# Strassen's products for 24 of the 32 column blocks of a decoder layer's up projection

## The chip, the cores and the metric

The kernel runs on one core of a Trainium2 chip. The core has a matrix engine (TensorE, PE in the profile; its weight loads are PEld), a vector engine (VectorE, DVE), an engine for activations (ScalarE, ACT), a general one (GpSimd, POOL) and one that issues transfers (SyncE, SP). Each takes its own queue in order and waits for the others by semaphores. The metric is the time of one execution in microseconds (us) of device time.

## The reference

One layer of a hybrid decoder trunk: 512 tokens, width 1024. A mixer (a gated recurrent group and a sparse attention group behind one input projection) is followed by a feed-forward part, which alone is touched here:

```python
x = x + (1.0 + g1[:, None, :]) * rms_norm(y, post_norm_mix[l])
h = modulate(rms_norm(x, pre_norm_mlp[l]), sh2, sc2)
y = jnp.square(jax.nn.relu(h @ w_ff1[l])) @ w_ff2[l]
x = x + (1.0 + g2[:, None, :]) * rms_norm(y, post_norm_mlp[l])
```

h is 512 x 1024, w_ff1 (up) 1024 x 4096, w_ff2 (down) 4096 x 1024, all float32.

## The kernel before

**Precision.** Every float32 operand is split into two parts of a shorter type, hi (a rounded copy) and lo (the remainder), and `mm3` multiplies hi x hi, hi x lo and lo x hi into the same sum. `split_f32` makes the parts: a copy (on ACT or DVE) and a subtraction (on DVE or POOL). So each weight and each activation costs work on those engines before PE can use it.

**Order.** The kernel first runs its Python once with a clock of estimated costs (`Clocks`), in which streams of work (`Stream`, `run_streams`) are interleaved. This records one node for each instruction. `flush` then issues the nodes in the order that the string PLAN gives, two characters a node. Where an instruction has several possible engines (`choose`, by way of `either` and `copy`), a letter of PLACE for its stream decides: a for ACT, d for DVE, p for POOL. The letters of a stream are used up in the order in which the choices are recorded; WS is the weights' stream, TH the transposes' one, UF the first up blocks, UP the up stage, DN the down stage.

**Weights.** `Weights` holds jobs in order. Each loads 512 KB into one of 4 raw buffers and splits it into one of 4 slots of hi and lo (PART_BUFS). A job with `make` takes two slots. A slot is given back when its user drops it.

**Up projection.** h is normalised in two pairs of token tiles (256 tokens each), transposed (`turn_h`) and split into h2 and h2l, 8 tiles of 128 rows of the width. A column block f is 128 of the 4096 columns; its result is 128 x 512 (columns by tokens), the sum over 8 k-tiles of three matmuls of 512 columns. The first four blocks run in `up_first`, half the tokens at a time while the rest of the mixer ends, so in matmuls of 256 columns. The other 28 follow in `up`. `relu2` takes relu from PSUM on ACT and squares on POOL or DVE, and for the pairs below 28 also makes two sums for the down projection.

**Down projection.** It already uses Strassen's method in Winograd's form for 14 pairs of row blocks (NJ): `first_pair` and `first_ones` make the activations' and weights' combinations of the first four products, `second_pair` and `second_ones` those of the other three; four plain blocks (28 to 31) end it. All activations' parts come from `part()`, in a pool that opens when h2 is closed.

**Beside it.** `ada_row(5, ...)`, the stream G2, makes the row of the last gate: eight loads into the two `ar` tiles, two DVE steps on each, into accT.

The matmuls have line 315 in the profile, transposes 318, ACT's operations 325, all operations chosen between DVE and POOL 357, loads 399.

Of the kernel before, what the change touches and what calls it, by code (L numbers as in the profile page):

```python
# [6 lines left out]
F32 = mybir.dt.float32  # L7
# [43 lines left out]
PAIRS = (0, 1)  # L51

# [6 lines left out]
    '###*#+#-#&#(#v#3#6#8#9#:#M#P#R#U#X#?#E#H#W#^#$#)#%#,#.#/#0#L#4#1$&#{#2#7#<#K#N#Y#[#_#a#d#q#w$.$0$1$7'  # L59
    '$8$=$D$G$J$O$P$S#5#@#C#S$X#c#J#Q#V#b#k%>#O#Z#]#h#e$w#T#p#s$)$2%8#f#i#l#n#|$#$($+$9$:$<$>$?$A$B$C$H$E'  # L60
    '$U$F#t$3$5$@$Q$K$T$]#A$N#x$6$Y$j$`$W$V$Z$d$m$a$s$_$o$g$t$z%,$}$r${$b$M$[$l$p$c$e$i$n$q$~%)$-$;$R%#%$'
    '%-%1%(%%%7%*%A%9%2%0%F%:%L%=%6%4$|$k$u%+$v$^$f$h$y%.%3%D$x%/%j%O%M%c%?%@%C%P%N%e%V%G%I%R%`%h%X%Z%]%J'
    '%<%H%g%r%E%S%T%[%^%f%n%&%5%m%l%s%i&$%u%k%q%~%o&&%{%|&,&2&1&)&#%}%d%W%a%w%b%K%U%Y%_%p%v&-%B%Q&z&.&5&<'
    '&/&+&*&I&6&B&;&F&D&L&7&J&A&N&Q&0%y&%%x%z&3&4&G&9&M%t&(&v&f&h&T&Y&O&S&g&j&U&[&R&^&u&l&V&]&a&b&8&P&W&>'
    '&?&H&K&Z&_&q&@&X(#&x&o&m&i&|(9(*&y&n($&~(?(:(%(/(((A(L&c&C&p&d&e&s&t&w&}()&`&k&r(;(,(1(3(C(N(=(-(4(7'
    '(D(P(Q(Y(5(>(G(U#I(y(k)1)*(<(8(E(B(@(F(O(V#G-u#~$%(.(R&:&=(f(~);)o(H(S(M(Z(`(d(h(v)R(s(K)&)e)`(b(o(X'
    '(^)6(u(m&E&{(&(|(+)V(0)I)a*4)F)x)d*=*f+P*8*l*?*y*;*s*i+G+W,K+E,)+(+V+u,`-.([(j(l(n(a(i(t(w(z(2(6(p(q'
    '(r(}(x({)$)%)+).)#)5):)A)/)0)<)=)C(I(J(T)9)@)i#;#=#>#B#D#F#`#g#j#m#o#r(W(](_#u#z#}$$$*$,$/$4(c(e(g$I'
    '#y$L%;)))(),)-)3)4)7)8)>)?)D)E)G)J)K)L)N)S)k)t*#)B)H)P)[)^)_)b)c)f)u)})~*$*&*)*-*/*0*3*6*7*<*A*C*E)M'
    ')O)X)Z)Q)T)U)W)g)Y)]*%*.*5)q)r)v)w)h)j)n)p)z*Q*U*_)y){)|*()s***1*2*c+&+-+@+3+>*L*N*O*Y*F*P*S*T*m+I*9'  # L70
    '*:*>*@*B*D*G*H*J*K*R*V*W*X*j*k*p*r*v*w*z*}+#+%+*+/+5+9+`+n+w*a*b*e*h*q*x*{*|+$*~+}*Z*]*d*n*o*t*u+++,'
    '+4+6+7+8+:+=+?+A+D+F+H+J+K+L+U+Y,%,0,G)l)m*,*+*^*[+)+1+2+o,R,L,g,d+B+M+O+Q+R+S+T+X+Z+[+]+^+c+e+g+k+p'
    '+t+{,*,+,,,-,.,4,X-P/#,D,t0#09+a+b+j*I*M*`*g+l+m+r+_+h+v-G+s+y+~,$,&,(,1,3,5,7,9,:,=,O,],_,a,c,h,o,v'
    ',}+;+<,<,N,8,A,>,S+.+0+N+x+d+|+f+i-%-,-1-E-6-:-2-C-H,?,@,B,C,E,H,P,Q,T,U,V,Y,Z,e,f,i,k,m,s,u,x,z,{,~'
    '-(-4-;-j-$-&-*---0-5-7-<->,J,W,[,l,^,|,b,w-@-F-I+q+z,/,q,6,;,2,F-+-9-k-p-y-A-?-=-c-J-K-M-Q-R-V-W-[-^'
    '-e-h-i-o-w.,.S-B-D-N-O-S-m-Y-Z-|.&-T-U-`-b-g-q-v-x-{...m.{,n,p-)-/-#-X-~.#.%,I,M,j-L.3.6.7.8.9.G.Y/N'
    '0f.Q.T.V.W.X.a.d/(/./>.f.y0a-_-z.*.1.J.L.u.}/$.(.).-.<.A.H.2.B.M.x-3-8-a-s-]-d,r,y-f.$.0.;.@.P.I.?.R'
    '.C.O.Z._.q/-/1/4/;/G-l-n.+.:.//&-r-t-}//.].^.`.n/+/3/,/5/7/8/=/U.D.g.i.o.k.r.5.K.U.z/9/?/s/i/Q/C/E/V'
    '/:/J/M/O/H/K/R/[/W/p/q/x/*/0/A/_/L/Z.b.e/B/I/y/{0(0=0@/h/~0$0%0*0I/e/j/k/w0d0m/X/]/d/u/a/g/P/b/f/o/}'
    '0)0.050?03070+0R0^0_0g0N0P0p0r1*1+16170&000G0M18191~2W211,1;1=1>1@1H1113151D1N1h0K0Q0S0Z1O1P1Q1Y1S1T'  # L80
# [1631 lines left out]
```

## Time and profile before

| | us |
|---|---|
| median of 3 runs | 623.78 (623.05 to 623.98) |
| the profiled execution, its own time | 624.71 |
| its span, first to last instruction | 622.9 |
| mean granted TensorE clock, share of full | 0.994 |

Time outside the span is start and end of the program. The profile gives for each engine its busy time and share of the span. Rows of the order of time have start, duration, engine, line, operation, output and inputs by the program's names, shapes and a count; in square brackets stands how long the engine was idle before and what released it. Rows of a stretch of time (A:B) have the length, the busy time of PE, PEld, DVE, ACT and POOL with counts, the granted clock, the share of the transfer engines and GB/s. The busy times of instructions that overlap are counted once, while the mean duration of a group counts each in full. Matmuls are pipelined: the duration of one is longer than the distance to the next.

### The profile page before, as it was taken

The numbers are of one execution on the slowest core, as the hardware profiler recorded it, in microseconds if no ns is written. First come the engines' busy times: TensorE is split into PE (matmuls) and PEld (weight loads), VectorE is DVE, ScalarE is ACT, GpSimd is POOL, SyncE is SP. The second block draws the span as 40 slices with busy tenths as digits, with TensorE's granted clock in tenths as the row PEclk, the third lists the DMA queues.
The fourth block names the chain that finished last, engine by engine and source line by source line (L and its number), as shares of the span: only waits on it lengthen the run. The fifth ranks groups of instructions, "written<-read, shape, count | busy, mean of one in ns | idle before, by whom it ended". The sixth has DMA issues, their size and how long they took to land.

```text
span 622.9 us, 8887 instructions
## 1 busy us (share of the span) xinstructions
PE 599.3 (96%) x3072; PEld 499.8 (80%) x3072; DVE 500.1 (80%) x972; ACT 340.7 (55%) x699; POOL 204.5 (33%) x206
## 2 busy tenths in 40 slices
PE   6999999999889999999999999999998999999993
PEld 6888889967678889789888888888786788888883
DVE  5998989899998989886675617536699999998867
ACT  6546217899999999875312111121374666656412
POOL 5004012445536648323234456414400000230253
PEclk9999999999999999999999999999998999999998
DMA  8996895150019120007442322422223343443403
GB/s 352 378 321 241 318 382 193 71 209 27 17 69 351 59 105 11 1 2 253 182 174 68 124 79 68 135 86 84 68 85 128 120 137 123 153 168 103 135 1 135
DMA packets 26837, 89.03 MB, mean 143 GB/s; under 512 B 2980, under 2 KB 3236, under 8 KB 26792
## 3 DMA queue, kind: packets, MB, share of 16 engines
q1 hardware_dynamic: 26648, 88.40, 39.9%
q8 instruction: 24, 0.39, 0.3%
q14 instruction: 21, 0.17, 0.1%
q10 hardware_dynamic: 144, 0.07, 0.0%
HBM read 86.36 MB, written 2.10 MB: 142 GB/s over the span
## 4 chain that ended last, share of the span: by engine, by line
PE 88%; ACT 5%; DVE 4%; DMA 1%; issue 1%; POOLq 0%; POOL 0%; ACTq 0%; DVEq 0%
PE f L315 45%; PE s L315 17%; PE pv L315 13%; PE tp L315 9%; PE tp L318 4%; ACT h L325 1%; ACT r L325 1%; DVE lo_D L357 1%; DMA raw_d<-in_wd 1%; DVE r L357 1%; DMA r<-in_x 1%; ACT L325 1%; ACT p L325 1%; ACT junk L325 1%; DVE fl L357 0%
## 5 line engine op out<-in xcount | busy, mean ns | idle before, releaser
L315 PE MATMUL f<-h2l,hi_f 128*128 128x512 f32 x224 | 83.3, 389 | 0.0
L315 PE MATMUL f<-h,lo_f 128*128 128x512 f32 x224 | 83.2, 392 | 0.0
L315 PE MATMUL f<-h,hi_f 128*128 128x512 f32 x224 | 83.0, 391 | 0.0
L325 ACT ACTIVATE fT<-f 128x512 f32<-128x512 f32 x28 | 16.7, 595 | 98.0 <-PE f L315 98.0
L315 PEld LDWEIGHTS f<-h,hi_f 128*128 128x128 f32 x224 | 42.0, 188 | 10.3 <-ACT fT L325 1.6
L315 PEld LDWEIGHTS f<-h,lo_f 128*128 128x128 f32 x224 | 42.0, 188 | 9.0 <-issue 0.2
L315 PEld LDWEIGHTS f<-h2l,hi_f 128*128 128x128 f32 x224 | 42.1, 188 | 8.6
L325 ACT ACTIVATE p<-p,mx 128x32 f32<-128x32 f32 (+4 forms) x96 | 45.1, 472 | 0.9 <-DVE mx L357 0.7
L315 PE MATMUL f<-hi_o,h 128*128 128x512 f32 x128 | 44.7, 406 | 0.9 <-ACT h L325 0.8
L357 POOL TENSOR_TENSOR fT<-fT 128x512 f32<-128x512 f32 (+1 forms) x23 | 25.9, 1124 | 57.5 <-ACT fT L325 50.4
L357 DVE TENSOR_TENSOR lo_f<-raw_f,hi_f 128x1024 fp32r<-128x1024 f32 x23 | 35.5, 1559 | 9.4 <-ACT hi_f L325 9.1
L357 DVE CAST hi_f<-raw_f 128x1024 fp32r<-128x1024 f32 x17 | 13.1, 769 | 37.1 <-PE f L315 32.5
L315 PE MATMUL s<-K,Q 128*128 128x288 f32 (+4 forms) x128 | 36.1, 338 | 2.4 <-DVE mx L357 1.7
L315 PE MATMUL pv<-pt,V 128*128 128x256 f32 x160 | 37.6, 305 | 0.0
L318 PE MATMUL tp<-ident,p 128*128 128x128 f32 x192 | 36.5, 274 | 0.9 <-DVE pt L357 0.9
L357 DVE TENSOR_TENSOR fT<-fT 128x512 f32<-128x512 f32 (+1 forms) x23 | 22.9, 1010 | 17.4 <-ACT fT L325 16.8
L357 DVE TENSOR_TENSOR pt<-tp,pt 128x512 fp32r<-128x512 f32 (+1 forms) x56 | 33.6, 607 | 2.6 <-ACT pt L325 1.6
L357 POOL TENSOR_SCALAR p<-p,den 128x32 f32<-128x32 f32 (+4 forms) x37 | 31.0, 847 | 10.3 <-DVE den L357 9.1
L357 POOL TENSOR_TENSOR lo_f<-raw_f,hi_f 128x1024 fp32r<-128x1024 f32 x9 | 23.3, 2593 | 25.4 <-PE f L315 10.4
L357 POOL TENSOR_TENSOR lo_e<-silb,hi_e 128x512 fp32r<-128x512 f32 x1 | 1.3, 1327 | 89.1 <-ACT hi_e L325 89.1
L325 ACT ACTIVATE junk<-r 128x1024 bf16<-128x1024 f32 (+1 forms) x20 | 17.7, 886 | 23.5 <-DVE r L357 22.5
L315 PEld LDWEIGHTS pv<-pt,V 128*128 128x128 f32 x160 | 27.2, 189 | 3.7 <-issue 0.7
(333 smaller groups left out, 1844.5 us busy)
## 6 DMA issues: line engine op xcount, KB each, us to landing
raw_f<-in_wf SPq DMA_DIRECT2D x32, 512.0 KB, 3.4
p<-in_ada_a SPq DMA_DIRECT2D x16, 512.0 KB, 6.3
p<-in_ada_t SPq DMA_DIRECT2D x16, 512.0 KB, 5.9
ar<-in_ada_r SPq DMA_DIRECT2D x16, 512.0 KB, 3.6
raw_d<-in_wd SPq DMA_DIRECT2D x14, 512.0 KB, 3.3
raw_e<-in_wd SPq DMA_DIRECT2D x14, 512.0 KB, 3.4
r<-in_x SPq DMA_DIRECT2D x8, 512.0 KB, 6.9
raw_c<-in_wc SPq DMA_DIRECT2D x8, 512.0 KB, 5.2
```

The costliest lines, as they stand in the source:

```text
L315: lambda: self.nc.tensor.matmul(out, lhs, rhs, start=start, stop=stop))
L318: self.issue("pe", 0.109, [out], [src], lambda: self.nc.tensor.transpose(out, src, ident))
L325: return "act", cost, lambda: self.nc.scalar.activation(out, src, func, scale=scale, bias=bias, **kw), func
L357: return eng, cost, lambda: fn(out, *args, **kw), None
```

## The change

Blocks 4 to 27 of the up projection, 24 of 32, are computed in twelve pairs by Strassen's method on 2 x 2 blocks: the two column blocks of a pair are one way, the halves of the 1024 rows of the weights (and of h) the other, the halves of the tokens the third. Seven products of 4 k-tiles and 256 tokens take the place of eight.

- `whole(A{j})` loads the first column block of a pair, B{j} the second; the jobs B and C (C loads nothing) make seven pieces of weights of 512 columns, with four additions between them, and each takes two slots.
- `turn_h` and `up_first` make the sums S1 to S4 of the activations and split them; S4's lo part and the raw of S3 live in the two `ar` tiles, S1 and S2 in two r8 tiles, S3 in a tile that `last`, the result of the last four blocks, takes over.
- `up_pair` runs the products in the order of UP_WAY, each into a bank of 256 columns, and joins them with one ACT copy and seven DVE additions from PSUM; relu and squares are then taken from SBUF, mostly on ACT.
- In `ada_sum` the G2 loads (part 5) are issued when needed instead of one ahead.
- The first two parts of the down projection's activations come from an r8 tile (`early`, `kept`), and the pool of the others has 9 instead of 6 buffers.
- PLAN and PLACE are new throughout.

```diff
+    def up_ones(j):
+        def make(raw, pieces):
+            a, b = W.loaded[f"A{j}"], raw
+            (xh, xl), (yh, yl) = pieces
+            lo, hi = half(0), half(1)
+            split_f32(clk, xh[:, lo], xl[:, lo], a[:, lo], usual="a")
+            either("tensor_add", a[:, lo], a[:, lo], b[:, lo])
+            split_f32(clk, xh[:, hi], xl[:, hi], a[:, lo], usual="a")
+            either("tensor_add", a[:, lo], a[:, lo], b[:, hi])
+            split_f32(clk, yh[:, lo], yl[:, lo], a[:, lo], usual="a")
+            either("tensor_add", b[:, lo], b[:, lo], b[:, hi])
+            split_f32(clk, yh[:, hi], yl[:, hi], b[:, lo], usual="a")
+            return ()
+        return make
+
+    def up_twos(j):
+        def make(raw, pieces):
+            a, b = W.loaded[f"A{j}"], W.loaded[f"B{j}"]
+            (xh, xl), (yh, yl) = pieces
+            lo, hi = half(0), half(1)
+            split_f32(clk, xh[:, lo], xl[:, lo], a[:, hi], usual="a")
+            either("tensor_add", a[:, lo], a[:, lo], a[:, hi])
+            split_f32(clk, xh[:, hi], xl[:, hi], a[:, lo], usual="a")
+            split_f32(clk, yh[:, lo], yl[:, lo], b[:, hi], usual="a")
+            return f"A{j}", f"B{j}"
...
+    for j in range(HALVES // 2, NJ):
+        whole(f"A{j}", inp["wf"][2 * j], split=False)
+        whole(f"B{j}", inp["wf"][2 * j + 1], make=up_ones(j))
+        W.add(f"C{j}", 0, [], make=up_twos(j))
...
-            if k % 2 == 0 and k // 2 + 1 < KD // 2:
+            if k % 2 == 0 and k // 2 + 1 < KD // 2 and part == 2:
                 fetch(k // 2 + 1)
+            if k % 2 == 0 and k and part == 5:
+                fetch(k // 2)
...
+        for k2 in range(2):
+            yield lambda: 0.0
+            either("tensor_sub", sums[k2], hfs[1, k2], hfs[1, k2 + 2])
+            split_f32(clk, blocks[0][:, 0, half(k2)], blocks[0][:, 1, half(k2)], sums[k2], usual="a")
+        for k2 in range(2):
+            yield lambda: 0.0
+            either("tensor_sub", sums[k2], sums[k2], hfs[0, k2])
+            split_f32(clk, blocks[1][:, 0, half(k2)], blocks[1][:, 1, half(k2)], sums[k2], usual="a")
+        for k2 in range(2):
+            yield lambda: 0.0
+            if not k2:
+                ffs["raw3"] = ar_tile()
+                clk.hold(ffs["raw3"])
+            either("tensor_sub", ffs["raw3"][:, half(k2)], hfs[0, k2], hfs[1, k2])
+            either("tensor_add", hfs[0, k2 + 2], hfs[0, k2 + 2], sums[k2])
...
+    UP_WAY = (("A11", 0, 0, "f"), ("S1", 0, 1, "pv"), ("S2", 2, 0, "tp"), ("A12", 4, 0, "s"), ("S3", 2, 1, "f"),
+              ("A22", 4, 1, "tp"), ("S4", 6, 0, "pv"))
+
+    def up_pair(j):
+        x, y = fT[2 * j], fT[2 * j + 1]
+        lo, hi = slice(0, 256), slice(256, 512)
+        for what, piece, n, tag in UP_WAY:
+            yield lambda: max(W.when(f"B{j}" if piece < 4 else f"C{j}"), bank_free(tag))
+            w = W.get(f"B{j}" if piece < 4 else f"C{j}")[piece % 4:piece % 4 + 2]
+            ps = bank(tag)[:, :256]
+            for k in range(4):
+                mm3(ps, [z[:, n * 512 + k * P:n * 512 + k * P + P] for z in w], ffs[what][k], k == 0, k == 3)
+            if what == "A11":
+                clk.copy(x[:, hi], ps, usual="a")
+            elif what == "S1":
+                p5 = ps
+            elif what == "S2":
+                dve("tensor_add", y[:, lo], ps, x[:, hi])
+            elif what == "A12":
+                dve("tensor_add", x[:, lo], ps, x[:, hi])
+            elif what == "S3":
+                dve("tensor_add", y[:, hi], ps, y[:, lo])
+                dve("tensor_sub", y[:, lo], p5, y[:, lo])
+            elif what == "A22":
+                dve("tensor_add", x[:, hi], ps, y[:, hi])
+                dve("tensor_sub", y[:, hi], p5, y[:, hi])
+                relu(x)
+                squares(2 * j)
+            elif what == "S4":
+                dve("tensor_add", y[:, lo], ps, y[:, lo])
+                relu(y)
+                squares(2 * j + 1)
+                sums(j)
+        W.drop(f"B{j}")
+        W.drop(f"C{j}")
...
+    early = r8()
+    early = early.rearrange("p a b -> p (a b)")[:, :2048].rearrange("p (a b) -> p a b", a=4).bitcast(F32R)
+    kept = [[early[:, 2 * k + z, :] for z in range(2)] for k in range(2)]
+
     def part():
-        return [small(an, z, 6, [P, 512], F32R) for z in ("fh", "fl")]
+        return kept.pop(0) if kept else [small(an, z, 9, [P, 512], F32R) for z in ("fh", "fl")]
```

The letters of PLACE for the twelve pairs' weights (job B: four splits with three additions between, eleven letters; job C: three splits and one addition, seven letters) and for the up stage read, in the order of the jobs:

```
B2 addaddaddad C2 addadad   B3 addaddaddap C3 adpadad   B4 addaddaddad C4 apdddad
B5 addapdadpad C5 addadad   B6 apdaddaddad C6 addadad   B7 addapdadpad C7 adddpad
B8 addaddaddad C8 apdadad   B9 addapdadpad C9 addadad   B10 ddpaddaddad C10 addadap
B11 addadpaddap C11 addaddd B12 adpaddaddad C12 addadad B13 addaddaddap C13 adpadad
UP: adad aaddaadd, pairs 2 to 13 (copy, relu, square, relu, square, sum, sum):
aaaaadp aaaaadd aaaaadp aaaaapd aaaaapd aaaaadd daaaapd aaaaapd aaaadpp daaaapd aaadadp aaaaadd, aaaa
```

More of the change, by code (lines that the diff above doesn't have):

```diff
@@ L51 @@
 PAIRS = (0, 1)
+HALVES = 4
 TABLES = {AF.Exp: ("exp",), AF.Tanh: ("exp", "sigmoid", "gelu"), AF.Sigmoid: ("sigmoid",), AF.Sqrt: ("sqrt",),
@@ L64 @@
[L64 to L68, printed above, removed]
@@ L465, in action @@
     def action(self):
-        if self.l < len(self.jobs) and len(self.raw_live) < RAW_BUFS:
+        if self.l < len(self.jobs) and (len(self.raw_live) < RAW_BUFS or not self.jobs[self.l][2]):
             return "load"
@@ L487, in load @@
         name, _, loads, _ = self.jobs[self.l]
+        if not loads:
+            self.l += 1
+            return
         raw = self.clk.tile(self.raws, "raw", RAW_BUFS, [P, 1024], F32, f"raw_{name}")
@@ L497, in split @@
         name, n, _, split = self.jobs[self.s]
-        raw = self.loaded[name]
+        raw = self.loaded.get(name)
         c = self.clk
@@ L735, in block_kernel @@
                 whole(f"o{hf_}{n}{k2}", inp["wo"][4 * hf_ + 2 * n + k2], gains=gains)
-    for f in range(NF):
+    def up_ones(j):
[22 more added lines that the diff above has]
+            return f"A{j}", f"B{j}"
+        return make
+    for f in range(HALVES):
+        whole(f"f{f}", inp["wf"][f])
+    for j in range(HALVES // 2, NJ):
+        whole(f"A{j}", inp["wf"][2 * j], split=False)
+        whole(f"B{j}", inp["wf"][2 * j + 1], make=up_ones(j))
+        W.add(f"C{j}", 0, [], make=up_twos(j))
+    for f in range(2 * NJ, NF):
         whole(f"f{f}", inp["wf"][f])
@@ L1468, in turn_h @@
             events.add(f"t{2 * th + 1}")
-    HALVES = 4
+        sums = [h_tile(F32) for k in range(2)]
+        blocks = [r8().rearrange("p a b -> p (a b)")[:, :2048].rearrange("p (z c) -> p z c", z=2).bitcast(F32R)
+                  for k in range(2)]
+        ffs["S1"], ffs["S2"] = [[[blocks[e][:, z, k * 256:k * 256 + 256] for z in range(2)] for k in range(4)]
+                                for e in range(2)]
+        for k2 in range(2):
[13 more added lines that the diff above has]
+            either("tensor_add", hfs[0, k2 + 2], hfs[0, k2 + 2], sums[k2])
     def up_first():
@@ L1489, in up_first @@
         ffs["first"] = pss
+        hi = slice(256, 512)
+        ffs["A11"], ffs["A12"] = [[[z[k][:, 0:256] for z in (h2, h2l)] for k in range(k0, k0 + 4)] for k0 in (0, 4)]
+        ffs["A22"] = [[z[k][:, hi] for z in (h2, h2l)] for k in range(4, 8)]
+        yield lambda: 0.0 if TH.done else INF
+        s4l = ar_tile().rearrange("p (k c) -> p k c", k=4).bitcast(F32R)
+        clk.hold(s4l)
+        ffs["S4"] = [[z[:, k, :] for z in (s4h, s4l)] for k in range(4)]
+        for k2 in range(2):
+            two = slice(2 * k2, 2 * k2 + 2)
+            split_f32(clk, s4h[:, two, :], s4l[:, two, :], hfs[0, k2 + 2].rearrange("p (k c) -> p k c", k=2), usual="a")
     TH, UF = Stream(clk, turn_h(), "TH"), Stream(clk, up_first(), "UF")
@@ L1496, in block_kernel, with squares, sums @@
     ff = ctx.enter_context(tc.tile_pool(name="ff", bufs=1, side="right", reuse_waits="tile"))
-    fT = [clk.lone(ff, [P, 512], F32, name=f"fT{f}") for f in range(NF)]
+    fT = [clk.lone(ff, [P, 512], F32, name=f"fT{f}") for f in range(2 * NJ)]
     t2 += fT[0:2 * NJ - 4:2]
     fS = [clk.lone(ff, [P, 256], F32, name=f"fS{j}") for j in range(NJ)]
-    def relu2(f, ps):
-        act(fT[f], ps, AF.Relu)
-        either("tensor_mul", fT[f], fT[f], fT[f], usual="p")
-        if f % 2 and f < 2 * NJ:
-            a, b, c = fT[f - 1], fT[f], fS[f // 2]
+    def squares(f):
+        t = fT[f]
+        clk.choose([t], [t], "p", clk.act_way(t, t, AF.Square), clk.elem_way("dve", "tensor_mul", t, t, t),
+                   clk.elem_way("pool", "tensor_mul", t, t, t))
+    def sums(j):
+        if j < NJ:
+            a, b, c = fT[2 * j], fT[2 * j + 1], fS[j]
             lo, hi = slice(0, 256), slice(256, 512)
@@ L1509, in relu2 @@
             either("tensor_sub", a[:, hi], a[:, lo], a[:, hi])
-    def up():
+    def relu2(f, ps):
+        act(fT[f], ps, AF.Relu)
+        squares(f)
+        if f % 2:
+            sums(f // 2)
+    UP_WAY = (("A11", 0, 0, "f"), ("S1", 0, 1, "pv"), ("S2", 2, 0, "tp"), ("A12", 4, 0, "s"), ("S3", 2, 1, "f"),
[32 more added lines that the diff above has]
+        W.drop(f"C{j}")
@@ new lines, in relu @@
+    def relu(t):
+        clk.choose([t], [t], "a", clk.act_way(t, t, AF.Relu),
+                   clk.elem_way("dve", "tensor_scalar", t, t, 0.0, None, op0=ALU.max))
+    def up():
+        third = clk.tile(ff, "f3", 1, [P, 2048], F32R, "third")
+        third = [third[:, k * 512:k * 512 + 512] for k in range(4)]
+        ffs["S3"] = [[third[2 * z + k // 2][:, k % 2 * 256:k % 2 * 256 + 256] for z in range(2)] for k in range(4)]
+        for k2 in range(2):
+            split_f32(clk, third[k2], third[2 + k2], ffs["raw3"][:, half(k2)], usual="a")
+        clk.release(ffs["raw3"])
@@ L1512, in up @@
         for f in range(HALVES):
             relu2(f, ffs["first"][f])
-        for f in range(HALVES, NF):
+        for j in range(HALVES // 2, NJ):
+            yield from up_pair(j)
+        last = clk.tile(ff, "f3", 1, [P, 2048], F32, "last")
+        fT.extend(last[:, k * 512:k * 512 + 512] for k in range(4))
+        for f in range(2 * NJ, NF):
             for k in range(KD):
```

249 lines of the change are left out of this document (137 added, 112 removed).

## The prediction

> **What bounds the kernel now.** I read the page first, then busy time by stretch, then the chain of work that ended last, then the groups and the order of VectorE's instructions.
>
> ```profile
> PE 599.3 (96%) x3072; PEld 499.8 (80%) x3072; DVE 500.1 (80%) x972; ACT 340.7 (55%) x699; POOL 204.5 (33%) x206
> ```
>
> TensorE carries the span, so work taken from it can shorten the time; VectorE, at 80%, comes next. Which of the two ends last differs by stage:
>
> ```profile
> core 0: us, PE busy (x) PEld busy (x) DVE busy (x) ACT busy (x) POOL busy (x), PEclk, DMA share, GB/s
> ...
> 292.00:296.60 4.60, 4.60 (x33) 4.03 (x32) 1.86 (x3) 1.87 (x3) 0.69 (x1) 1.00 0.59 225
> 296.60:451.00 154.40, 153.97 (x675) 125.50 (x673) 85.89 (x85) 31.71 (x47) 64.16 (x44) 1.00 0.32 106
> 451.00:463.00 12.00, 12.00 (x54) 9.62 (x53) 11.86 (x23) 8.67 (x17) 0.00 (x0) 1.00 0.30 102
> 463.00:490.00 27.00, 23.62 (x93) 17.90 (x92) 25.21 (x43) 14.73 (x23) 0.00 (x0) 0.94 0.34 108
> 490.00:534.50 44.50, 44.50 (x195) 36.00 (x194) 44.09 (x67) 29.74 (x47) 0.08 (x1) 1.00 0.45 150
> ```
>
> 296.6 to 451 is the up projection after its first four blocks: PE never rests, DVE is busy 85.89 of 154.4 us (56%). 451 to 534.5 is the first half of the down projection: DVE is busy 81.16 of 83.5 us (97.2%), and PE lost 3.4 us there. So DVE is free in the stage that is changed and is the bound in the one behind it.
>
> ```profile
> 273.51 2.16 PE pv L315 x18
> ...
> 278.28 2.40 PE s L315 x20
> ...
> 296.62 28.68 PE f L315 x126
> ...
> 326.16 124.00 PE f L315 x544
> ```
>
> In the chain a matmul of 512 columns takes 124.00/544 = 0.228 us, one of 256 columns (the first four blocks, half the tokens each, a weight load before every one) 2.16/18 = 0.120 us: 0.006 over half.
>
> **PE's gain.** A pair of column blocks took 2 x 24 matmuls at 0.228 = 10.94 us. Strassen takes 7 products x 4 k-tiles x 3 = 84 at 0.120 = 10.08. Twelve pairs save 12 x 0.86 = 10.3 us. The PE-paced end of the up projection is thus 440.7 instead of 451.
>
> **What DVE gets.** Its prices are taken from start to start where it runs without a pause:
>
> ```profile
> 456.67 0.76 DVE L357 TENSOR_TENSOR fS<-fT,fS 128x256 f32<-128x256 f32 x2
> 457.34 1.22 DVE L357 TENSOR_TENSOR lo_D<-raw_D,hi_D 128x1024 fp32r<-128x1024 f32 x1
> 458.48 0.42 DVE L357 TENSOR_TENSOR fl<-fS,fh 128x256 fp32r<-128x256 f32 x1
> 458.81 1.22 DVE L357 TENSOR_TENSOR lo_D<-raw_d,hi_D 128x1024 fp32r<-128x1024 f32 x1
> ...
> 460.28 0.68 DVE L357 TENSOR_TENSOR fl<-fT,fh 128x512 fp32r<-128x512 f32 x1
> 460.89 1.22 DVE L357 TENSOR_TENSOR lo_D<-raw_D,hi_D 128x1024 fp32r<-128x1024 f32 x1
> ```
> ```profile
> L357 DVE TENSOR_TENSOR pt<-tp,pt 128x256 fp32r<-128x256 f32 x16 | 6.7, 420 | 0.5 <-ACT pt L325 0.2
> ```
> ```profile
> 284.72 3.83 DVE L357 SCALAR_TENSOR_TENSOR accT<-ar,sil,accT 128x512 f32<-128x512 f32 x4
> ...
> 291.28 0.54 DVE L357 TENSOR_SCALAR h<-tp,a,s 128x256 f32<-128x256 f32 x1
> 294.64 0.70 DVE L357 CAST hi_f<-raw_f 128x1024 fp32r<-128x1024 f32 x1 [2.83 <-PE pv L315]
> ...
> 301.06 0.48 DVE L357 TENSOR_SCALAR accT<-ar,sil 128x512 f32<-128x512 f32 x1
> 301.57 1.54 DVE L357 SCALAR_TENSOR_TENSOR accT<-ar,sil,accT 128x512 f32<-128x512 f32 x2
> ```
>
> So 1024 columns take 1.14 us, 512 take 0.61, 256 take 0.335 (two in 0.67; with one input in PSUM the duration, 420 ns, is the same), an accT step 0.77, a cast of 512 half of 0.70. Counting the letters of PLACE in the order of the jobs:
> - twelve pairs: of 11 subtractions and additions of 512 columns each, 113 of 132 go to DVE (19 to POOL): 68.9 us; 4 casts 1.4; 7 additions from PSUM a pair, 84 x 0.335 = 28.1; 14 of the 24 sums for the down projection 4.7; four odd ones 1.9. Together 105.0, or 8.75 us for a pair of 10.08.
> - the blocks S1 to S4 of the activations: 8 sums and 8 remainders of 512 columns, all on DVE, 16 x 0.61 = 9.8.
> - sums of the first four blocks 1.3; weights of the four plain blocks at the end 4 x 1.14 = 4.6.
> - the row G2: 14 x 0.77 + 2 x 0.48 + 2 x 0.61 = 13.0. Four of its steps ran from 284.72 on so far, ahead of the stage. Now S4 keeps one of the two ar tiles and the raw of S3 the other until the up stage has begun, so all of it falls behind.
> - the down projection's first half, unchanged: 14 x (3 x 0.61 + 2 x 1.14 + 0.61 + 4 x 0.335) = 84.8 against 24 x 0.228 = 5.47 of PE each (76.6): DVE-bound by itself, which is why it leans on work done ahead. The first part of its second half, due at the boundary: 1.14 + 3 x 0.61 + 0.335 = 3.3.
>
> Sum 221.8 us, from 292 on: S1 to S4 need the last transposed rows (291.28 plus 0.54), and B2's pieces the slots of f0 and f1, neither much earlier.
>
> **POOL beside DVE.** POOL keeps 19 ops of 512 and 10 of 256 columns in the pairs, some 27 us instead of 64.
>
> ```profile
> 402.38 0.73 POOL L357 TENSOR_TENSOR fS<-fT,fT 128x256 f32<-128x256 f32 x1 [1.83 <-DVE fT L357]
> ...
> 420.00 1.04 POOL L357 TENSOR_TENSOR fT<-fT 128x512 f32<-128x512 f32 x1 [10.19 <-ACT fT L325]
> ```
> ```profile
> L357 DVE TENSOR_TENSOR lo_f<-raw_f,hi_f 128x1024 fp32r<-128x1024 f32 x19 | 30.5, 1626 | 8.9 <-ACT hi_f L325 8.6
> L357 DVE TENSOR_TENSOR fT<-fT 128x512 f32<-128x512 f32 x15 | 17.6, 1187 | 16.8 <-ACT fT L325 16.8
> ```
> ```profile
> L357 DVE TENSOR_TENSOR lo_D<-raw_d,hi_D 128x1024 fp32r<-128x1024 f32 x12 | 14.6, 1218 | 0.3 <-ACT hi_D L325 0.3
> ...
> L357 DVE TENSOR_TENSOR fl<-fT,fh 128x512 fp32r<-128x512 f32 x16 | 10.9, 684 | 0.3 <-ACT fh L325 0.3
> ```
>
> The first two groups are of the up stage, the last two of the down stage, where POOL rests. Beside POOL the same shapes take 19 x 0.408 + 15 x 0.503 = 15.3 us more, 0.24 us per POOL us at a DVE share of 56%; scaled to 97% it is 0.42. I take the middle, 0.33: 27 x 0.33 = 8.9 us, with ends 0 and 27.
>
> **The sum.** 221.8 + 8.9 = 230.7 us of DVE work. At the share that the down stage shows (97.2%) it takes 237.3 us and ends at 292 + 237.3 = 529.3; now it ends where the first sums of the results begin:
>
> ```profile
> L357 DVE TENSOR_TENSOR fT<-pv,r x2: 673/675/677, 534.5 to 535.1; 128x512 f32<-128x512 f32 x2
> ```
>
> So 5.2 us come out of 10.3: half of PE's gain is given back, because DVE becomes the pace from 292 to 529. It shows at two places: the first pair's last product could start at 296.6 + 6 x 12 x 0.120 = 305.2, while DVE owes it S1 to S4 (9.8), B2 and C2 (11 x 0.61 = 6.7) and five sums (1.7), so 310.2; and at the end less weight work is ready when the down projection begins.
>
> **Edits costed at nothing.**
>
> ```profile
> L325 ACT ACTIVATE fh<-fT x31: 610/619/636, 450.5 to 588.0; 128x512 fp32r<-128x512 f32 x31
> ```
> ```profile
> SPq L399 <- DVE accT L357: 16.4, 2, 8.4
> ```
> ```profile
> ar<-in_ada_r SPq DMA_DIRECT2D x16, 512.0 KB, 3.6
> ```
>
> ACT takes 80 casts, most relus and squares and the copies of A11: some 12 x 11 x 0.62 = 82 us with eight casts for S and the plain blocks' work 95 of 144: free, but each remainder waits for its cast. PSUM: a bank is used again a pair (10 us) later; nothing. The G2 loads now have one free buffer and come on demand: 3.6 us from issue to landing, twice two accT steps apart. I take 0, since other DVE work can stand between; the far end is seven exposed loads, 25 us. In SP's queue such a load waits for the accT step (it did twice, 16.4 us) with A and B raws queued behind; they run a pair, 10 us, ahead. No load is added. The early homes (one r8 tile, nine more bufs instead of six) let first_pair(0), 0.61 + 4 x 0.335 = 1.95 us, be split before the up stage ends: nothing while DVE is the bound, at most the 3.4 us that PE lost if it isn't. The rest of the kernel has the same instructions in another order: PLAN has 5451 entries instead of 4731, and 12 pairs x 58 (36 matmuls, 14 ops on weights, 8 on results) + 24 for S are just these 720. I take 0 for that; 622.9 - 599.3 = 23.6 us of PE idle bound it, and I allow 2 us to either side.
>
> **Rivals.**
> 1. PE stays the pace: DVE finds its work early enough, as PE did at DVE shares over 95% from 490 to 534.5. Then 10.3 us go, and up to 3.4 of the down stage: 613.5 down to 610. Against it: 221.8/(440.7 + 76.6 - 292) = 98% DVE without any contention. Chance 0.18.
> 2. Slower by the port: a POOL op stops DVE outright.
>
> ```profile
> 398.17 2.39 POOL L357 TENSOR_TENSOR lo_f<-raw_f,hi_f 128x1024 fp32r<-128x1024 f32 x1 [6.55 <-PE f L315]
> ```
> ```profile
> 398.19 2.91 DVE L357 TENSOR_TENSOR fT<-fT 128x512 f32<-128x512 f32 x1 [0.16 <-ACT fT L325]
> ```
> A 0.68 us op took 2.91, begun with a POOL op of 2.39. If every POOL us stops DVE while it is at work with two SBUF inputs (70% of the pairs' DVE time: 73.6 of 105.0), 27 x 0.7 = 19 us: 240.8/0.972 = 247.7, end at 539.7, 5.2 us slower: 629. It decides from 14 us of stretch on (242.5 x 0.972 - 221.8), 0.52 per POOL us. Against it: 0.24 seen. Chance 0.22. [...]
> 3. No change: DVE, which takes its queue in order, stands before the ar loads. One and a half of seven exposed (3.6 us each) eat the 5.2 us: 624. Chance 0.12.
>
> **How the numbers follow.** The profiled execution (624.71 us, span 622.9) stands 0.93 over the median of 623.78; forecast 624.71 - 5.2 = 619.5 there, 618.6 at the median, chance 0.48, its own range 615 to 622.5. Over 0.2% (1.25 us, about what a measurement of this kernel tells from no change) faster: 0.48 + 0.18 = 0.66; same 0.12; slower 0.22. The range goes from rival 1's better end to rival 2: 610 to 629.
>
> **What would show it.** Right: 1008 matmuls of 256 columns at 0.120 apart; DVE share in the up stage from 56% to over 90%, with PE waits released by DVE that were not there, early in the stage and again where the down projection begins; POOL's busy time about halved. Wrong: PE without waits through the pairs (rival 1), DVE groups of 512 columns well over 0.9 us in the mean (rival 2), DVE idle before accT released by DMA (rival 3), or 256-column matmuls at 0.130, which alone would undo the gain.

## The result and the profile after

| | before | after |
|---|---|---|
| median on the same chip, us | 623.53 (4 runs) | 617.64 (615.99 to 618.04, 4 runs) |
| ratio, 95% interval | | 0.9901 (0.988 to 0.9921) |
| span of the profiled execution, us | 622.9 | 616.3 |

The change takes 5.9 us off; 618.6 was forecast. Of PE's gain of some 10 us more than half is left, though not by the account of the prediction alone (see the part on why it was right). In the kernel after, matmuls have line 334, transposes 337, ACT's operations 344, those on DVE and POOL 376; an edit shifts these numbers (335, 345 and 377, or 327, 337 and 369, are the same lines). First the page's busy times:

```profile
PE 590.4 (96%) x3504; PEld 514.7 (84%) x3504; DVE 554.3 (90%) x1152; ACT 406.1 (66%) x824; POOL 167.4 (27%) x189
```

PE does 8.9 us less, DVE 54.2 more, POOL 37.1 less. By stretch (pairs; plain blocks; first half of the down projection; second half):

```profile
core 0: us, PE busy (x) PEld busy (x) DVE busy (x) ACT busy (x) POOL busy (x), PEclk, DMA share, GB/s
292.00:426.80 134.80, 132.87 (x1063) 129.19 (x1063) 126.99 (x235) 84.23 (x149) 36.40 (x30) 1.00 0.36 122
426.80:446.80 20.00, 20.00 (x90) 16.55 (x89) 18.16 (x29) 9.47 (x15) 3.71 (x3) 1.00 0.48 159
446.80:528.70 81.90, 79.29 (x343) 63.55 (x342) 81.18 (x129) 54.57 (x89) 1.00 (x1) 1.00 0.40 127
528.70:606.50 77.80, 77.80 (x345) 64.19 (x344) 63.39 (x104) 34.11 (x58) 19.61 (x11) 1.00 0.32 107
```

In the pairs DVE is at 94% and PE at 98.6%; what room is left lies with ACT (62%) and POOL (27%). From 292 to 528.7 DVE is busy for 126.99 + 18.16 + 81.18 = 226.3 us of 236.7 (95.6%); the forecast was 230.7 of 237.3. The first sums of the results, in the tile view, begin at 528.7 (forecast 529.3, before 534.5):

```profile
L376 DVE TENSOR_TENSOR fT<-pv,r x2: 682/683/684, 528.7 to 529.3; 128x512 f32<-128x512 f32 x2
```

The matmuls in the order of time stand 0.12 apart, as forecast, except behind a wait:

```profile
338.37 0.28 PE L334 MATMUL tp<-h2l,hi_C 128*128 128x256 f32 x1
338.49 0.28 PE L334 MATMUL tp<-h,lo_C 128*128 128x256 f32 x1
338.61 0.28 PE L334 MATMUL f<-h2l,hi_B 128*128 128x256 f32 x1
339.69 0.39 PE L334 MATMUL pv<-s4h,hi_C 128*128 128x256 f32 x1 [0.80 <-DVE fT L376]
```

**Where the time went.** The table is worked out from the starts of all matmuls in the traces. "Up" runs from the first up matmul to the last plain one, "down" from there to the last matmul of that half; "lost" is what the distances between PE's starts have over 0.12 or 0.228 us, in the up stage behind its first four blocks and in down. The profiled executions of these thirteen kernels reach the first up matmul at 265 to 268 us (before 267.79, after 267.39), so stage lengths tell small differences better than ends.

| | median, us | ratio (95%) | up | down | lost in up | lost in down |
|---|---|---|---|---|---|---|
| before | 623.5 | | 182.0 | 84.3 | 1.0 | 7.5 |
| after | 617.64 | 0.9901 (0.988 to 0.9921) | 179.3 | 82.3 | 6.8 | 4.6 |
| e1_no_g2 | 615.9 | 0.9879 (0.9862 to 0.9895) | 179.2 | 82.3 | 6.7 | 4.6 |
| e14_half | 628.18 | 1.008 (1.0064 to 1.0097) | 190.1 | 82.9 | 17.8 | 5.1 |
| e2_double | 640.02 | 1.0264 (1.0248 to 1.0281) | 201.0 | 82.4 | 28.6 | 4.8 |
| e5_before_double | 624.62 | 1.0019 (1.0002 to 1.0037) | 184.6 | 83.1 | 3.6 | 6.3 |
| e3_no_pool | 623.7 | 1.0001 (0.9989 to 1.0012) | 185.3 | 82.4 | 12.9 | 4.6 |
| e10_three | 616.68 | 0.9886 (0.9871 to 0.9901) | 178.4 | 82.3 | 5.9 | 4.6 |
| e4_g2_pool | 623.49 | 1.0002 (0.9991 to 1.0014) | 184.2 | 83.2 | 11.6 | 5.5 |
| e8_down_pool | 626.42 | 1.0052 (1.0038 to 1.0065) | 179.4 | 92.3 | 6.9 | 14.4 |
| e11_d_light | 617.05 | 0.9899 (0.9885 to 0.9912) | 179.2 | 81.9 | 6.8 | 4.2 |
| e12_order | 616.23 | 0.9885 (0.9866 to 0.9904) | 178.4 | 82.5 | 6.0 | 4.6 |
| e13_order_light | 615.57 | 0.9868 (0.9847 to 0.9889) | 178.3 | 80.8 | 5.9 | 3.1 |

Ratios stand against the kernel before on the same chip. From before to after: up 2.7 us shorter, down 2.0, the rest 1.5; the first up matmul starts 0.4 earlier, which makes the 6.6 us between the two spans. In up, by the distances from each start to the next, matmuls of 512 columns take 130.4 us less (678 became 104, those of the mixer that fall into it included). Those of 256 columns take 126.5 us more: 192 became 1200, and 1008 x 0.120 are 121.0, so 5.5 are pauses. The transposes of the last rows take 1.2 us more. In down, PE's loss fell by 2.9; 0.9 of it goes to six matmuls that run there now, four of the second half and two for the gate row. The four, not a faster second half, are most of the 1.5 us of the rest.

### The profile page after: what moved, and what is told of

Its sections match the earlier page's. It is cut to its first block, busy times and chain, and to the rows that moved or that the text cites. A ratio compares the mean times of both kernels' runs of the same rounds, so it can differ in the third digit from the quotient of the medians.

```text
span 616.3 us, 10061 instructions
## 1 busy us (share of the span) xinstructions
PE 590.4 (96%) x3504; PEld 514.7 (84%) x3504; DVE 554.3 (90%) x1152; ACT 406.1 (66%) x824; POOL 167.4 (27%) x189
## 4 chain that ended last, share of the span: by engine, by line
PE 76%; DVE 13%; ACT 7%; issue 2%; DMA 1%; POOL 0%; DVEq 0%; ACTq 0%
PE f L334 26%; PE s L334 18%; PE pv L334 16%; PE tp L334 12%; PE tp L337 4%; DVE fT L376 3%; DVE fl L376 1%; ACT p L344 1%; DVE lo_B L376 1%; DVE lo_C L376 1%; DVE lo_D L376 1%; ACT h L344 1%; ACT r L344 1%; ACT L344 1%; ACT junk L344 1%
## 5 line engine op out<-in xcount | busy, mean ns | idle before, releaser
L344 ACT ACTIVATE hi_B<-raw_A 128x512 fp32r<-128x512 f32 x35 | 22.1, 631 | 28.5 <-DVE raw_A L376 21.0
L344 ACT ACTIVATE fT<-fT 128x512 f32<-128x512 f32 x50 | 30.6, 623 | 2.7 <-DVE fT L376 2.2
L344 ACT ACTIVATE junk<-r 128x1024 bf16<-128x1024 f32 (+1 forms) x20 | 17.8, 888 | 16.8 <-DVE r L376 16.8
L337 PEld LDWEIGHTS tp<-ident,p 128*128 128x128 f32 x192 | 24.5, 140 | 4.8 <-issue 1.1
L376 DVE CUSTOM_DVE_ANT_0 p<-p,silb 128x1024 f32<-128x1024 f32 x23 | 27.9, 1221 | 0.1
L334 PEld LDWEIGHTS f<-hi_o,h 128*128 128x128 f32 x128 | 23.2, 189 | 5.4 <-ACT h L344 1.4
L334 PE MATMUL f<-lo_o,h 128*128 128x512 f32 x64 | 25.9, 410 | 0.0
L334 PEld LDWEIGHTS s<-K,Q 128*128 128x128 f32 x128 | 22.4, 188 | 3.4 <-issue 0.7
L334 PE MATMUL tp<-r,hi_B 128*128 128x256 f32 x96 | 23.0, 285 | 0.1
L334 PE MATMUL pv<-r,hi_B 128*128 128x256 f32 x96 | 22.5, 284 | 0.0
L376 DVE TENSOR_TENSOR lo_B<-raw_A,hi_B 128x512 fp32r<-128x512 f32 x32 | 22.0, 686 | 0.5 <-ACT hi_B L344 0.2
```

The lines of the kernel that those rows point to most:

```text
L334: lambda: self.nc.tensor.matmul(out, lhs, rhs, start=start, stop=stop))
L337: self.issue("pe", 0.109, [out], [src], lambda: self.nc.tensor.transpose(out, src, ident))
L344: return "act", cost, lambda: self.nc.scalar.activation(out, src, func, scale=scale, bias=bias, **kw), func
L376: return eng, cost, lambda: fn(out, *args, **kw), None
```

## Experiments

Theory 1 is the prediction's: DVE's total work is the pace. Its rival, theory 2: PE is the pace, and single waits, which the fixed order of the queues makes, cost it the rest. Theory 3, formed after the first four runs: the up stage is PE's with single waits, some of them made by operations of POOL beside which one of DVE takes longer (1.79 us instead of 0.68 at 337 in after; the expectations call this the lock or the port, and the runs show the durations alone); the first half of the down projection is bound by DVE by itself. Theory 4 came later and is told where it is put to the test. Each kernel is the one after with one edit, unless told otherwise.

### Less and more work for DVE in the up stage

e1_no_g2 leaves the 14 accT steps of G2 out. The node is recorded, so that the order stays, but issues nothing:

```diff
+                clk.times = 0 if part == 5 else 1
                 either("scalar_tensor_tensor", acc, raw, sil[:, k:k + 1], acc, op0=ALU.mult, op1=ALU.add)
+                clk.times = 1
```

> The changed kernel with the 14 accumulating steps of the row G2 (0.77 us each on VectorE) left out, everything else in its place; the last gate is wrong. Theory 1 (VectorE is the pace from 292 to 529 us, 226 of 237 us busy): 10.8 us less of its work ends that stretch 5 to 10 us earlier, 608 to 613 us, the top of TensorE's idle time there being about 11 us. Theory 2 (TensorE waits on chains from engine to engine, VectorE's total doesn't matter): 0 to 1 us, 617.

The median is 1.7 us lower, but the interval overlaps that of after, and the profile has both stages at the same length. The stretch of the pairs, and what DVE waited for in it, here and in after:

```profile
298.20:426.50 128.30, 126.31 (x1011) 122.76 (x1010) 116.02 (x216) 78.56 (x141) 35.14 (x30) 1.00 0.38 127
```
```profile
DVE fT L377 <- PE tp L335: 5.5, 7, 1.6
```
```profile
DVE fT L376 <- PE tp L334: 2.2, 3, 1.5
```

DVE is busy for 116.02 instead of 120.70 us of the same length (eight of the 14 steps ran there), and waits 5.5 us for PE's products instead of 2.2. The time set free sits behind additions that wait for PE, and nothing behind them ran ahead of them in DVE's fixed order. Theory 1 as the prediction put it falls; theory 2 holds in this direction.

e2_double computes two remainders of each job C a second time (24 x 512 columns), e14_half one of them (12 x 512), e5_before_double does the same to the kernel before, with half of each remainder of blocks 4 to 27:

```diff
-            split_f32(clk, xh[:, hi], xl[:, hi], a[:, lo], usual="a")
-            split_f32(clk, yh[:, lo], yl[:, lo], b[:, hi], usual="a")
+            split_f32(clk, xh[:, hi], xl[:, hi], a[:, lo], usual="a", times=2)
+            split_f32(clk, yh[:, lo], yl[:, lo], b[:, hi], usual="a", times=2)
```

> The changed kernel with two of the seven remainders of each pair's weights computed twice (24 more subtractions of 512 columns, about 0.61 us each, nearly all on VectorE). Theory 1: 14.6 us more of VectorE's work at 96% busy cost 12 to 15 us, 630 to 633 us. Theory 2: 0 to 4 us, at most 622.

> Half of e2_double's dose: in each of the twelve pairs one remainder of job C, not two, is computed a second time, 12 x 0.61 = 7.3 us more DVE work; DVE is idle for 7.8 of the 134.8 us of the pairs. If only the free time counts (a queue at its capacity), it fits and costs 0 to 2 us against 617.6. If the 22 us of e2_double are a slope of 1.5 us for each us added, some 11: 628 to 629.

> The control for e2_double: the kernel before, with the second 512 columns of the remainder of each weight block 4 to 27 of the up projection computed a second time on DVE, the same 24 x 0.61 = 14.6 us of DVE work in the same stage. Where DVE has a slack of 44% (before), the extra work should cost 0 to 2 us: 623 to 626, and PE should lose little more than 1 us between the last of the first blocks and the end of the up projection. If it costs 15 us or more here too, then it is the place of the extra operation (it delays a piece that PE waits for), not the fullness of DVE, that made 22 us in e2_double.

Rows of the stretch from the end of the first four blocks to the end of the pairs: after, e14_half, e2_double.

```profile
298.20:426.60 128.40, 126.47 (x1011) 122.79 (x1010) 120.70 (x224) 78.85 (x140) 36.40 (x30) 1.00 0.38 127
```
```profile
296.20:435.40 139.20, 130.29 (x1010) 123.54 (x1009) 131.80 (x235) 78.77 (x140) 37.37 (x31) 1.00 0.35 116
```
```profile
298.20:448.30 150.10, 132.05 (x1010) 125.06 (x1009) 142.34 (x246) 78.95 (x141) 39.53 (x32) 0.99 0.33 108
```

DVE's busy time grows by 11.1 and 21.6 us, the stretch by 10.8 and 21.7: the work that was added was paid in full, and DVE's share stays at 94 to 95%. That 7.3 us cost 10.8, and 14.6 cost 21.7 (e2_double is 7 us above theory 1's range), comes from the operations: 12 more at 0.684 us, the duration of one, are 8.2, and others grew longer (the 29 of lo_B<-raw_A from 686 to 756 ns in the mean). What DVE's operations took over the usual duration of their shape (0.684, 0.42 or 1.22 us) is 4.4 us in after, 8.2 in e14_half and 11.1 in e2_double; 3.8 of the 4.4 stand beside POOL, and in e3_no_pool, with POOL's operations of the pairs on DVE, the largest groups of 512 columns have means of 684 to 691 ns. In e2_double the granted clock of this stretch was 0.99 in the mean, so its 21.7 us aren't DVE's alone; in e14_half and in after it was 1.00.

The control, the kernel before with the extra work and without, from the end of the first four blocks to the end of the up stage:

```profile
294.90:450.90 156.00, 153.69 (x674) 125.35 (x673) 96.48 (x106) 31.01 (x45) 64.61 (x44) 1.00 0.31 105
```
```profile
296.30:449.80 153.50, 153.50 (x675) 125.50 (x673) 85.05 (x82) 31.21 (x45) 64.16 (x44) 1.00 0.32 107
```

As many operations of the same shape add 11.4 us of busy time to a DVE at 56%, and the stretch grows by 2.5 (the median by 1.25, interval 0.1 to 2.3). So it was the fullness of DVE that counted here (94 against 56%), not the operation. Upward, theory 1 holds. The two theories are not rivals but two limits that meet: PE at 98.5% and DVE at 94% of one stretch.

### POOL beside DVE

e3_no_pool puts all 29 POOL operations of the pairs on DVE, e10_three only three, beside which a remainder was stretched (to 1.8 us) just before a wait of PE. Both change letters of PLACE alone:

```diff
-C4 apdddad  B6 apdaddaddad  C8 apdadad
+C4 addddad  B6 addaddaddad  C8 addadad
```

> The changed kernel with the 29 operations that POOL has in the twelve pairs given to VectorE by their letters. If a POOL operation stops VectorE for as long as it saves it (the port rival), 0 us or faster. If it costs VectorE only the 4 us of stretch that its groups show, VectorE gets 19 x 0.61 + 10 x 0.335 - 4 = 11 us more and the time rises by 8 to 11 us, 626 to 629.

> The kernel after, with three POOL operations of the pairs on DVE instead (the ones beside which a DVE remainder was stretched to 1.8 us just before PE's waits at 317.9, 338.6 and 361.0 us; the two largest were 0.95 and 0.94). Local waits by the lock (theory 3): these waits go, 1.5 to 2.5 us less: 615 to 616. If DVE's total load were the pace: 3 x 0.61 = 1.8 us more work, 1 to 2 us slower: 618.6 to 619.6. If the waits come from the order alone, about 617.6.

In e3_no_pool the pairs end 5.4 us later, PE waiting for the additions fT:

```profile
PE pv L327 <- DVE fT L369: 4.4, 8, 1.1
```

```profile
297.60:432.00 134.40, 128.46 (x1010) 123.33 (x1009) 129.60 (x253) 79.07 (x141) 1.59 (x1) 1.00 0.35 121
```

So POOL's help is worth 6 us in all; what DVE's operations took longer beside it doesn't eat it, though it is less than the 8 to 11 expected. DVE has 8.9 us more to do in a stretch that is 6.0 longer, at a share of 96.4%: here a part of the idle time of after was used, so 94 to 95% was not a ceiling. One by one it differs. VectorE's and GpSimd's rows of after, at the largest wait of the pairs, and then VectorE's of e10_three at the same place:

```profile
336.70 0.42 DVE L376 TENSOR_TENSOR fT<-f,fT 128x256 f32<-128x256 f32 x1
337.04 1.79 DVE L376 TENSOR_TENSOR lo_C<-raw_B,hi_C 128x512 fp32r<-128x512 f32 x1
338.76 0.87 DVE L376 TENSOR_TENSOR fT<-pv,fT 128x256 f32<-128x256 f32 x2
```
```profile
336.99 1.30 POOL L376 TENSOR_TENSOR lo_B<-raw_A,hi_B 128x512 fp32r<-128x512 f32 x1 [0.16 <-ACT hi_B L344]
```
```profile
335.27 0.68 DVE L369 TENSOR_TENSOR lo_C<-raw_B,hi_C 128x512 fp32r<-128x512 f32 x1
335.87 0.42 DVE L369 TENSOR_TENSOR fT<-pv,fT 128x256 f32<-128x256 f32 x1
336.20 0.68 DVE L369 TENSOR_TENSOR lo_B<-raw_A,hi_B 128x512 fp32r<-128x512 f32 x1
```

POOL starts 0.05 ahead of DVE and ends at 338.29; DVE's 0.68 become 1.79, to 338.83, and the addition behind it, for which PE waits, starts 1.1 late. Without the POOL operation DVE has even the remainder that POOL had made done by then. PE's pauses there fall from 0.95 and 0.94 (at 361) to 0.32 and 0.52, and the up stage from 179.3 to 178.4, less than the 1.5 to 2.5 expected. The trace shows these 0.9 us; the ratios don't separate e10_three from after.

e4_g2_pool makes G2's steps as a scaling on ACT and an addition on POOL.

```diff
+                        nc.scalar.activation(raw, raw, AF.Copy, scale=col, bias=0.0)
+                        nc.gpsimd.tensor_add(acc, acc, raw)
```

> The changed kernel with the 14 accumulating steps of G2 as a scaling on ACT (0.62 us) and an addition on POOL (1.04 to 1.3 us) in place of one step on VectorE (0.77 us). Theory 1 with a weak port: VectorE is rid of 10.8 us and loses 1 to 3 us to POOL, 3 to 8 us faster, 610 to 614. Port rival: 14 x 1.3 = 18 us of POOL stop VectorE for more than the 10.8 us saved, 618 to 625. Theory 2: 617.

It is 6 us slower than after. PE's two largest waits from the pairs to the up stage's end, and the row of ACT behind the first of them:

```profile
PE f L334 <- ACT last L344: 2.3, 1, 2.3
PE s L334 <- POOL lo_C L376: 1.6, 1, 1.6
```
```profile
440.61 0.63 ACT L344 ACTIVATE silb<-raw_D 128x512 f32<-128x512 f32 x1 [3.96 <-DVE raw_D L376]
442.71 0.57 ACT L344 ACTIVATE last<-f 128x512 f32<-128x512 f32 x1
```

ACT stood for 3.96 us before a combination that DVE owed it, with a step of G2 and the copy `last`, which frees PE's bank, behind. POOL in turn came late with a remainder. But the queues are not all: DVE's operations took 12.0 us over their usual durations up to the end of the up stage, against 4.4 in after, and 623.5 lies in the range expected of the port rival. So 10.8 us of work taken off the full engine brought nothing, by POOL beside DVE and by longer queues of ACT and POOL together; this run doesn't part them.

### The first half of the down projection

Theory 3 was: this half is bound by DVE's 81 busy of 82 us alone, from wherever it starts. e8_down_pool moves one combination of each of its 14 jobs to POOL, e11_d_light leaves another one out, in the way of e1_no_g2:

```diff
+            clk.times = 0
             either("tensor_sub", a[:, half(1)], a[:, half(1)], a[:, half(0)])
+            clk.times = 1
```

> The kernel after, with one of the three 512-column weight combinations of the first half of the down projection (raw_D, 14 of them, 14 x 0.61 = 8.5 us of DVE) on POOL, which rests there. Theory 3 (the first half of the down projection is DVE-bound by its own 82 us, wherever it starts): PE lost 4.6 us there, so it ends 2 to 4 us earlier if POOL's ops (some 1.3 us each) stretch DVE by less than half of what they take over: 614 to 616. If the port lock eats it (each POOL op stops DVE for its 1.3 us, 14 x 1.3 = 18 us against 8.5 saved), it is 5 to 9 us slower: 622 to 627. If PE or waits by order are the pace there, 0: 617.6.

> The kernel after, with the 14 subtractions of 512 columns that make raw_d in first_ones left out (8.5 us less DVE work in the first half of the down projection; these 14 pieces of weights hold other numbers). Theory 3 (that half is DVE-bound by itself): it ends 3 to 4.5 us earlier, PE's loss of 4.6 us there nearly gone: 613 to 614.5. If order and buffers set its pace and not DVE's work: no change, 617.6.

Theory 3 falls with e11_d_light: 8.5 us less work, 0.4 us shorter. The row of the half, then what DVE and PE waited for:

```profile
447.00:528.90 81.90, 79.36 (x345) 64.05 (x344) 75.54 (x119) 54.49 (x90) 1.26 (x2) 1.00 0.40 132
```
```profile
DVE lo_D L377 <- ACT hi_D L345: 4.1, 5, 1.4
```
```profile
PE f L335 <- DVE lo_D L377: 2.0, 2, 1.5
PE f L335 <- ACT last L345: 0.6, 1, 0.6
```

DVE, which did not wait at all in after, now waits for ACT's casts, and PE's waits are those of after to the digit. The largest is for a remainder lo_D whose cast runs behind two other casts in ACT's queue (it ends at 470.95) and which itself stands behind other operations in DVE's (it starts at 471.72). e8_down_pool is 10 us longer there. POOL's group, and what DVE waited for:

```profile
L369 POOL TENSOR_TENSOR raw_D<-raw_D,raw_d 128x512 f32<-128x512 f32 x12 | 19.9, 1655 | 49.4 <-DMA raw_D<-in_wd 22.1 <-DVE raw_D L369 9.0 <-ACT hi_D L337 8.0
```
```profile
DVE raw_d L369 <- POOL raw_D L369: 7.6, 5, 2.9
```

POOL's operation takes 1.66 us where DVE takes 0.68, in the middle of a chain from load to remainder, and DVE stands before it. The loss can come from the chain or from DVE's operations taking longer beside POOL; this run doesn't part the two.

Theory 4: PE is the pace here too, and the order makes its waits. e12_order is e10_three with nine instructions elsewhere in the order: the copy of a last up result (4258) ahead of a cast, and, around job D4, one matmul, the combinations, cast and remainders (4429 to 4452) earlier.

```diff
+MOVES = ((4258, 4503), (4503, 4504), (4292, 4504), (4429, 4433), (4446, 4509), (4447, 4550), (4449, 4551), (4448, 4551), (4452, 4590))
+        for k, ahead_of in MOVES:
+            order.remove(k)
+            order.insert(order.index(ahead_of), k)
```

e13_order_light is e12_order with the edit of e11_d_light.

> e10_three with the same instructions and nine of them at other places in the order, around PE's two largest waits of the down projection's first half (0.75 us at 446.9 behind an ACT copy of the last up result, 1.73 us at 468.0 behind a remainder lo_D). Theory 4 (PE is the pace everywhere; what it loses are local waits made by the order of the queues, not by DVE's total): 1.5 to 2.3 us less than e10_three, 614.4 to 615.2. Theory 1 again (DVE's 81 busy of 82 us in that half are its pace): the waits come back later in the same half, 616 to 617.

> e12_order with the 14 subtractions for raw_d left out as in e11_d_light (8.5 us less DVE work; these 14 pieces of weights hold other numbers). Theory 4: the same as e12_order within 0.5 us. Theory 1: if e12_order brought less than 1.5 us, the lighter DVE brings the rest here, 614 to 615.

The two waits at which the moves aimed went (0.75 at the start to nothing, 1.73 to 0.15), but PE loses 4.6 us as before, in new waits at 452.9, 472.4 and 474.8, and the median, 616.23, lies where theory 1 had it. PE's waits of e12_order, then of e13_order_light, in this half:

```profile
PE f L334 <- DVE lo_D L376: 0.9, 2, 0.5
PE tp L334 <- DVE g2row L376: 0.9, 1, 0.9
PE s L334 <- ACT hi_D L344: 0.5, 1, 0.5
```
```profile
PE tp L335 <- DVE g2row L377: 0.9, 1, 0.9
PE f L335 <- DVE lo_D L377: 0.8, 2, 0.4
```

Less work alone gives 0.4 us, this other order alone nothing, both together 1.5 (82.3 to 80.8). The trace shows these; the ratios of e12_order and e13_order_light overlap, and the median of the latter, 615.57, lies in neither theory's range. So theory 4 falls as well when taken alone, as far as one other order can show it. The reading that fits is that a better order spends DVE time that isn't there (DVE is busy 81.5 of 82.3 us in e12_order), and that DVE time that is set free has no operation that may use it. The kernels e10_three and e12_order, which compute all of the reference, are ahead of before by 1.1% and of after by 1.0 to 1.4 us in the median; their intervals overlap with that of after. Other homes for the first two parts of the down projection's activations were not tried.

## Why the prediction was right, and where not

- **PE's gain, 10.3 us:** right. The distances in the records are 0.120 and 0.227, for 1008 and 576 matmuls 9.8 us.
- **DVE's total:** 230.7 us forecast, 226.3 measured, at a share of 97.2 and 95.6%; the end of the half 0.6 us early. That it agrees so well is partly luck. Of the 16 operations for S1 to S4 (9.8 us), twelve ran before 292: the last transposed rows came at 283.6, not at 291.3. POOL's stretch of DVE was put at 8.9 us and is 4.4, mostly in the groups below; POOL's own 29 operations took 35.1 us instead of 27 (most of 512 columns 1.30, not 1.04). Against both, the price of 0.61 for 512 columns was too low where operations depend on each other (0.72 in the rows below): some 38 distances of 0.70 us and more in the pairs make 4 us. Some 3 us stay open.

```profile
L376 DVE TENSOR_TENSOR lo_B<-raw_A,hi_B 128x512 fp32r<-128x512 f32 x32 | 22.0, 686 | 0.5 <-ACT hi_B L344 0.2
L376 DVE TENSOR_TENSOR raw_A<-raw_A,raw_B 128x512 f32<-128x512 f32 x21 | 14.9, 709 | 0.6
L376 DVE TENSOR_TENSOR lo_C<-raw_A,hi_C 128x512 fp32r<-128x512 f32 x21 | 14.8, 708 | 0.1
L376 DVE TENSOR_TENSOR lo_C<-raw_B,hi_C 128x512 fp32r<-128x512 f32 x11 | 9.7, 884 | 0.0
```
```profile
292.69 0.69 DVE L376 TENSOR_TENSOR ar<-h,s4h 128x512 fp32r<-128x512 f32 x1
293.29 0.69 DVE L376 TENSOR_TENSOR lo_B<-raw_A,hi_B 128x512 fp32r<-128x512 f32 x1
294.01 0.69 DVE L376 TENSOR_TENSOR raw_A<-raw_A,raw_B 128x512 f32<-128x512 f32 x1
```

  Two that have nothing to do with each other started 0.60 apart (292.69, 293.29); one that overwrites what the one ahead reads started 0.72 later (293.29, 294.01; 16 pairs of these two operations in the stretch, 0.716 to 0.727).
- **"DVE becomes the pace from 292 to 529":** the step that was half right. Upward it holds (e2_double, e14_half), downward it doesn't (e1_no_g2, e11_d_light): 10.8 of the 13.0 us of G2 in the sum could be left out and no stage got shorter. The change had brought the two engines to balance, and a sum of one engine's work said only what more would cost.
- **Where the loss shows:** wrong for the first pair. Its last product was put at 310.2, five us late; the matmuls of S4 begin at 299.9 without a wait. S4's last remainder was made at 292.69 (the rows above), and the new order mixes the products of a pair, which the prediction took one after the other:

```profile
L334 PE MATMUL pv<-s4h,hi_C x10: 283/283/283, 299.9 to 319.9; 128*128 128x256 f32 x10
```

  The loss is spread over all pairs, in some 40 pauses of 0.03 to 0.95 us. At the start of the down projection it is there, as foretold.
- **Down half:** its shortening by 2.0 us was not in the sum as such. Before, PE stood 1.96 us at 476 and then ran eight matmuls at half speed (below); after, it doesn't. In place of the 5.1 us that the prediction has given back stand two terms: PE's loss in the up stage grew by 5.8 us, its loss in down fell by 2.9. That they net near the forecast is luck too.
- **Costed at nothing:** the loads of G2 on demand are right: e1_no_g2 without the steps has the same stages, and DVE waits for no ar load in after. ACT, at 62% in the pairs, is free only on average: in e4_g2_pool and e11_d_light PE or DVE waited for one of its copies or casts.
- **Rival 2, the port:** seen in single places, as a whole not: e3_no_pool shows that POOL's 29 operations save 6 us. In the pair of rows at 337 DVE's 0.68 us became 1.79, while the group means of 686 to 709 show that most operations lost nothing. The records of the pairs say where POOL ran: beside 15 of 108 operations of 512 columns, nine of which took 679 to 693 ns and six 812 to 1793, and beside 64 of the 80 additions that take one input from PSUM, which were as long beside it (422 ns) as without (421). No run shows that POOL stops DVE for all of its time with two inputs in SBUF, the 0.7 in the 19 us of this rival; in its place 4.4 us of stretch were measured, 3.8 of them in those 15 operations. Whether the order puts POOL there or POOL waits for them isn't parted.

## What to carry to other kernels

When a change moves work from a bound engine to one with room, work out how full the second will be: here, at 94 to 95%, further work was paid in full or for the most part (10.8 and 21.7 us for 11.1 and 21.6 of busy time, and 6.0 for 8.9, against 2.5 for 11.4 in the kernel where it stood at 56%). At that balance neither less work nor the one other order that was tried helped alone; look for pairs of the two. And before you take a helper engine away because it disturbs, move single operations: three of 29 brought 0.9 us in the trace here, all 29 cost 6.

## What the runs showed of the hardware

**Behind most waits PE lost more than the wait.** In after, from 292 to 530, eight of the nine matmuls of 256 columns that start 0.28 us or more behind the one ahead stand 0.222 to 0.224 us from the next instead of 0.12 (339.69 to 339.91; at 420.79 it was 0.119). Of the four of 512 columns that start 0.45 us or more behind, three stand 0.335 or 0.336 from the next instead of 0.228 (473.07 to 473.40; at 449.81 it was 0.232):

```profile
473.07 0.50 PE L334 MATMUL f<-lo_D,fh 128*128 128x512 f32 x1 [1.52 <-DVE lo_D L376]
473.40 0.40 PE L334 MATMUL f<-hi_D,fh 128*128 128x512 f32 x1
473.64 0.39 PE L334 MATMUL f<-hi_D,fl 128*128 128x512 f32 x1
```

**Half speed behind one wait.** In the kernel before, behind the wait at 476:

```profile
478.21 0.69 PE L315 MATMUL s<-hi_D,fh 128*128 128x512 f32 x1 [1.79 <-ACT hi_D L325]
478.69 0.63 PE L315 MATMUL f<-hi_D,fh 128*128 128x512 f32 x1
479.12 0.63 PE L315 MATMUL pv<-lo_D,fh 128*128 128x512 f32 x1
479.55 0.63 PE L315 MATMUL pv<-hi_D,fl 128*128 128x512 f32 x1
```

The starts are 0.427 apart instead of 0.228 (1.96 us is the idle time by the starts; the row's 1.79 counts from a modelled end). The trace's record of the granted clock has it at 0.5 from 478.35 to 481.76, for 3.41 us. In after the granted clock of the same half is 1.00 (446.80 to 528.70). In e8_down_pool it was 0.96 in the mean of that half:

```profile
444.90:536.90 92.00, 83.25 (x343) 65.20 (x342) 83.75 (x121) 54.59 (x89) 21.02 (x14) 0.96 0.36 117
```

PE waited there 2.1 us once for an ACT copy and up to 2.0 for a remainder. What set the half speed off is not shown.
